# RMSNorm with GELU, one core: the first fill in three loads of 64 KB pieces, squares half a group ahead, and one store for the last group

## The chip, the cores and the metric

The kernel runs on one core of a Trainium2 chip. The metric is the device time of one execution in microseconds (us), fast runs only; a smaller number is better. "Faster" or "slower" asks for 2%, here 6.3 us. The profile of an execution covers its instructions from first to last (the span), some 1.8 us less than the time.

## The reference

x is 8 x 1024 x 2048 in float32: 8192 rows of 2048.

```python
rms = np.sqrt(np.mean(x ** 2, axis=-1, keepdims=True) + eps)
out = gamma * x / rms
return 0.5 * out * (1 + np.tanh(np.sqrt(2 / np.pi) * (out + 0.044715 * out ** 3)))
```

67.1 MB are read once and 67.1 MB written once. Nothing is reused but gamma.

## The kernel before

The rows are worked on in 16 groups of 512: each of 128 partitions holds four consecutive rows, 32 KB. Six buffers of that size (slots) go round: SyncE issues the loads, ScalarE squares the rows (accumulating a sum for each), GpSimd makes the inverse root from the four sums, VectorE multiplies by gamma in place, ScalarE applies GELU in place with the inverse root as its scale and issues the store. A load into a slot waits for the store that empties it.

```python
x3 = x...rearrange("(g p r) d -> g p r d", p=P, r=R)         # P = 128, R = 4
slot = [sbuf.tile([P, R, D], FP32, ...) for i in range(SLOTS)]   # 6
store_pieces = {
    0: [(R, [(0, NARROW), (NARROW, R * D)])],                # NARROW = 128 columns
    G - 1: [(1, [(r * D, r * D + D)]) for r in range(R)],    # the last group, row by row
}
...
for g in range(SLOTS):
    load(g)
...
for g in range(G + 1):
    if g < G:
        squares(g)                 # four ACTIVATE, one a row
        inverse_rms(g)             # six small GpSimd instructions
        scale(g)                   # one VectorE instruction (four for the last group)
    if g:
        gelu_store(g - 1)          # four ACTIVATE, then the store
        if g - 1 + SLOTS < G:
            load(g - 1 + SLOTS)
```

Squares of a whole group run ahead of the GELU of the one before. The first store is cut into a piece of 128 columns (512 bytes a partition) and the rest.

Of the kernel before, what the change touches and what calls it, by code (L numbers as in the profile page):

```python
# [1 line left out]

# [4 lines left out]

FP32 = mybir.dt.float32
ALU = mybir.AluOpType
ACT = mybir.ActivationFunctionType  # L10

P = 128
ROWS = 4
SLOTS = 6

GW = 32
CHUNK = 512

NARROW = 128


@with_exitstack
def kernel(
    ctx: ExitStack,
    tc: tile.TileContext,
    x: bass.AP,
    gamma: bass.AP,
    eps: bass.AP,
    out: bass.AP,
):  # L30




    nc = tc.nc
    D = x.shape[-1]
    R = ROWS
    eps_f = float(eps)
    x3 = x.rearrange("b s d -> (b s) d").rearrange("(g p r) d -> g p r d", p=P, r=R)
    o3 = out.rearrange("b s d -> (b s) d").rearrange("(g p r) d -> g p r d", p=P, r=R)  # L40
    G = x3.shape[0]

    sbuf = ctx.enter_context(tc.tile_pool(name="sbuf", bufs=1))
    psum = ctx.enter_context(
        tc.tile_pool(name="psum", bufs=1, space=bass.MemoryType.PSUM)
    )
    slot = [sbuf.tile([P, R, D], FP32, name=f"slot{i}") for i in range(SLOTS)]
    gamma_row = sbuf.tile([1, D // GW, GW + 4], FP32, name="gamma_row")
    ones = sbuf.tile([1, P], FP32, name="ones")
    warm = sbuf.tile([1, 1], FP32, name="warm")  # L50
    power = sbuf.tile([P, R], FP32, name="power")
    ssq = sbuf.tile([P, G, R], FP32, name="ssq")
    rstd = sbuf.tile([P, G, R], FP32, name="rstd")
    ms = sbuf.tile([P, R], FP32, name="ms")
    y = sbuf.tile([P, R], FP32, name="y")
    z = sbuf.tile([P, R], FP32, name="z")
    gamma_ps = psum.tile([P, D], FP32, name="gamma_ps")
    junk = psum.tile([P, D], FP32, name="junk")


    whole = [(R, [(0, R * D)])]
    store_pieces = {
        0: [(R, [(0, NARROW), (NARROW, R * D)])],
        G - 1: [(1, [(r * D, r * D + D)]) for r in range(R)],
    }
    scale_pieces = {G - 1: [(0, 1), (1, 1), (2, 1), (3, 1)]}

    def load(g):
        nc.sync.dma_start(out=slot[g % SLOTS], in_=x3[g])  # L69

    def squares(g):
        for r in range(R):
            nc.scalar.activation(  # L73
                out=junk,
                in_=slot[g % SLOTS][:, r, :],
                func=ACT.Square,
                accum_out=ssq[:, g, r : r + 1],
            )

    def scale(g):  # L80
        for r, n in scale_pieces.get(g, [(0, R)]):
            rows = slot[g % SLOTS][:, r : r + n, :]
            nc.vector.tensor_tensor(  # L83
                out=rows,
                in0=rows,
                in1=gamma_ps.unsqueeze(1).to_broadcast([P, n, D]),
                op=ALU.mult,
            )

    def inverse_rms(g):  # L90

        v = nc.gpsimd
        v.tensor_scalar(  # L93
            out=ms, in0=ssq[:, g, :], scalar1=1.0 / D, scalar2=eps_f,
            op0=ALU.mult, op1=ALU.add,
        )
        v.tensor_tensor(out=y, in0=ms, in1=power, op=ALU.pow)  # L97
        v.tensor_tensor(out=z, in0=y, in1=y, op=ALU.mult)  # L98
        v.tensor_tensor(out=z, in0=z, in1=ms, op=ALU.mult)  # L99
        v.tensor_scalar(  # L100
            out=z, in0=z, scalar1=-0.5, scalar2=1.5, op0=ALU.mult, op1=ALU.add
        )
        v.tensor_tensor(out=rstd[:, g, :], in0=z, in1=y, op=ALU.mult)  # L103

    def gelu_store(g):
        flat = slot[g % SLOTS].rearrange("p r d -> p (r d)")
        dst = o3[g].rearrange("p r d -> p (r d)")
        row = 0
        for n, stores in store_pieces.get(g, whole):
            for r in range(row, row + n):  # L110
                nc.scalar.activation(  # L111
                    out=slot[g % SLOTS][:, r, :],
                    in_=slot[g % SLOTS][:, r, :],
                    func=ACT.Gelu_apprx_tanh,
                    scale=rstd[:, g, r : r + 1],
                )
            row += n
            for a, b in stores:
                nc.scalar.dma_start(out=dst[:, a:b], in_=flat[:, a:b])  # L119

    with tc.manual_schedule():
        for k in range(0, D, CHUNK):
            nc.scalar.dma_start(
                out=gamma_row[:, k // GW : (k + CHUNK) // GW, 0:GW],
                in_=gamma[k : k + CHUNK].rearrange("(o a b) -> o a b", o=1, b=GW),
            )
        for g in range(SLOTS):
            load(g)
        nc.gpsimd.memset(power, -0.5)  # L129
        nc.vector.memset(warm, 0.0)  # L130
        nc.vector.memset(ones, 1.0)  # L131
        nc.scalar.activation(out=warm, in_=warm, func=ACT.Gelu_apprx_tanh)  # L132
        for k in range(0, D, CHUNK):
            nc.tensor.matmul(  # L134
                out=gamma_ps[:, k : k + CHUNK],
                lhsT=ones,
                rhs=gamma_row[:, k // GW : (k + CHUNK) // GW, 0:GW],
                start=True,
                stop=True,
            )  # L140
        for g in range(G + 1):
            if g < G:
                squares(g)
                inverse_rms(g)
                scale(g)
            if g:
                gelu_store(g - 1)
                if g - 1 + SLOTS < G:
                    load(g - 1 + SLOTS)


# [1 line left out]
_INS = ['x', 'gamma', 'eps']  # L153
_OUTS = [((8, 1024, 2048), 'float32')]

_NUMBERS = {'eps': 9.999999747378752e-06}


# [26 lines left out]
```

## Time and profile before

| | before |
|---|---|
| time | 317.41 us median of 3 (317.26 to 317.46) |
| span | 315.5 us |
| ScalarE / VectorE / GpSimd busy | 80% / 44% / 10% |
| DMA packets' time, share of 16 engines | 99.1% |
| first data packet, last packet | 1.73, 314.30 us |

The profile has one row for each instruction and a record for each packet that a DMA engine moved (queue, size, start, duration). Here a packet is one partition's contiguous run of bytes: 32 KB for a group's load. Each DMA also sends one 4-byte semaphore packet on each engine. The prediction shows the lines that matter, so here are only two marks that the change is going to shift. They are from the timeline of the kernel before (start, duration, engine, line, operation; in brackets the idle time before it), the first square and the last store:

```profile
13.47 1.88 ACT L73 ACTIVATE junk<-slot 128x2048 f32<-128x2048 f32 x1 [8.70 <-DMA slot<-in_x_dram]
...
297.05 0.34 ACTq L119 DMA_DIRECT2D out_dram<-slot  x1
```

The last store is issued at 297 us, but the queue is then so full that its last packet goes at 314.

### The profile page before, as it was taken

The page shows a single profiled execution, that of the slowest core. Times are in us where ns is not written, and L with a number is a line of the kernel's source. Part 1 is how long each engine was busy: PE and PEld are TensorE (multiplying, and loading weights), DVE is VectorE, ACT ScalarE, POOL GpSimd, SP SyncE. Part 2 cuts the span into 40 slices and gives each one's busy share as a digit, 9 for nine tenths or more (in the row PEclk, how much of TensorE's full clock was granted, in tenths as well). Part 3 has the DMA queues.
Part 4 walks back from the last instruction along what each step waited for, and adds up shares of the span by engine and source line. Part 5 has one row for each costly group of instructions (what it writes and reads, how often), then busy time and mean ns, then how long its engine had stood idle before and what let it go on. Part 6 is the DMA issues. An engine that isn't in the chain of part 4 may idle for free.

```text
span 315.5 us, 479 instructions
## 1 busy us (share of the span) xinstructions
PE 7.9 (3%) x8; PEld 2.1 (1%) x8; DVE 139.4 (44%) x21; ACT 251.2 (80%) x194; POOL 32.3 (10%) x101
## 2 busy tenths in 40 slices
PE   0810000000000000000000000000000000000000
PEld 0200000000000000000000000000000000000000
DVE  0028909091918282827328082370824609480000
ACT  1289999999999999989596895969959599598500
POOL 0020202020202020202020020200202002020000
DMA  8999999999999999999999999999999999999997
GB/s 329 404 461 403 459 413 396 453 406 462 403 461 407 457 407 458 411 453 416 449 428 440 432 432 432 432 440 424 446 416 453 411 453 411 453 415 449 416 418 314
DMA packets 5315, 134.25 MB, mean 426 GB/s; under 512 B 704, under 2 KB 832, under 8 KB 832
## 3 DMA queue, kind: packets, MB, share of 16 engines
q1 hardware_dynamic: 2304, 67.11, 49.7%
q10 hardware_dynamic: 3008, 67.12, 49.4%
q14 instruction: 3, 0.02, 0.0%
HBM read 67.12 MB, written 67.11 MB: 425 GB/s over the span
## 4 chain that ended last, share of the span: by engine, by line
ACT 38%; DMA 32%; another core or an unknown queue 18%; issue 5%; ACTq 1%; SPq 0%
ACT slot L111 21%; DMA slot<-in_x_dram 16%; ACT junk L73 16%; DMA out_dram<-slot 15%; ACTq L119 1%; SPq L69 0%; ACTq L111 0%; ACTq L73 0%
## 5 line engine op out<-in xcount | busy, mean ns | idle before, releaser
L83 DVE TENSOR_TENSOR slot<-slot,gamma_ps 128x8192 f32<-128x8192 f32 (+1 forms) x19 | 139.2, 7338 | 142.3 <-ACT junk L73 142.3
L73 ACT ACTIVATE junk<-slot 128x2048 f32<-128x2048 f32 x64 | 120.4, 1881 | 40.8 <-DMA slot<-in_x_dram 36.8
L111 ACT ACTIVATE slot<-slot,rstd 128x2048 f32<-128x2048 f32 x64 | 123.0, 1987 | 1.7 <-ACT slot L111 1.7
L93 POOL TENSOR_SCALAR ms<-ssq 128x4 f32<-128x4 f32 x16 | 3.1, 194 | 242.8 <-ACT junk L73 242.8
L97 POOL TENSOR_TENSOR y<-ms,power 128x4 f32<-128x4 f32 x16 | 16.1, 1009 | 1.3
L73 ACT ACTIVATION_READ_ACCUMULATOR junk<-slot 128x1 f32 x64 | 11.9, 186 | 0.0
L134 PE MATMUL gamma_ps<-gamma_row,ones 1*128 1x512 f32 x8 | 7.9, 1112 | 9.2 <-DMA gamma_row<-in_gamma_dram 9.2
L132 ACT ACT_TABLE_LOAD x1 | 1.3, 1283 | 3.3 <-issue 3.3
L99 POOL TENSOR_TENSOR z<-z,ms 128x4 f32<-128x4 f32 x16 | 3.2, 201 | 1.3
L103 POOL TENSOR_TENSOR rstd<-z,y 128x4 f32<-128x4 f32 x16 | 3.2, 200 | 1.3
L98 POOL TENSOR_TENSOR z<-y 128x4 f32<-128x4 f32 x16 | 3.2, 200 | 1.3
L100 POOL TENSOR_SCALAR z<-z 128x4 f32<-128x4 f32 x16 | 3.1, 195 | 1.4
L134 PEld LDWEIGHTS gamma_ps<-gamma_row,ones 1*128 1x128 f32 x8 | 2.1, 306 | 13.4 <-issue 8.7
L130 DVE MEMSET warm<- 1x1 f32 x1 | 0.1, 59 | 0.8 <-PEq L166 0.8
L132 ACT ACTIVATE warm<-warm 1x1 f32<-1x1 f32 x1 | 0.2, 203 | 0.0
L131 DVE MEMSET ones<- 1x128 f32 x1 | 0.2, 165 | 0.0
L129 POOL MEMSET power<- 128x4 f32 x1 | 0.1, 102 | 0.3 <-POOLq L166 0.3
L166 POOL MEMSET const-float32-0.0<- 128x1 f32 x1 | 0.1, 99 | 0.2 <-issue 0.2
L166 POOL MEMSET const-bfloat16-1.0<- 128x1 bf16 x1 | 0.1, 102 | 0.0
L166 POOL MEMSET const-uint8-127<- 128x1 uint8 x1 | 0.1, 102 | 0.0
L166 POOL MEMSET const-float32-1.0<- 128x1 f32 x1 | 0.1, 99 | 0.0
## 6 DMA issues: line engine op xcount, KB each, us to landing
slot<-in_x_dram SPq DMA_DIRECT2D x16, 4096.0 KB, 29.9
out_dram<-slot ACTq DMA_DIRECT2D x14, 4096.0 KB, 43.3
out_dram<-slot ACTq DMA_DIRECT2D x4, 1024.0 KB, 17.5
out_dram<-slot ACTq DMA_DIRECT2D x1, 4032.0 KB, 28.5
gamma_row<-in_gamma_dram ACTq DMA_DIRECT2D x4, 2.0 KB, 10.3
out_dram<-slot ACTq DMA_DIRECT2D x1, 64.0 KB, 14.4
```

What stands on the lines that cost most here:

```text
L73: nc.scalar.activation(out=junk, in_=slot[g % SLOTS][:, r, :], func=ACT.Square, accum_out=ssq[:, g, r : r + 1],)
L83: nc.vector.tensor_tensor(out=rows, in0=rows, in1=gamma_ps.unsqueeze(1).to_broadcast([P, n, D]), op=ALU.mult,)
L93: v.tensor_scalar(out=ms, in0=ssq[:, g, :], scalar1=1.0 / D, scalar2=eps_f, op0=ALU.mult, op1=ALU.add,)
L97: v.tensor_tensor(out=y, in0=ms, in1=power, op=ALU.pow)
L98: v.tensor_tensor(out=z, in0=y, in1=y, op=ALU.mult)
L99: v.tensor_tensor(out=z, in0=z, in1=ms, op=ALU.mult)
L100: v.tensor_scalar(out=z, in0=z, scalar1=-0.5, scalar2=1.5, op0=ALU.mult, op1=ALU.add)
L103: v.tensor_tensor(out=rstd[:, g, :], in0=z, in1=y, op=ALU.mult)
L111: nc.scalar.activation(out=slot[g % SLOTS][:, r, :], in_=slot[g % SLOTS][:, r, :], func=ACT.Gelu_apprx_tanh, scale=rstd[:, g, r : r + 1],)
L119: nc.scalar.dma_start(out=dst[:, a:b], in_=flat[:, a:b])
L132: nc.scalar.activation(out=warm, in_=warm, func=ACT.Gelu_apprx_tanh)
L134: nc.tensor.matmul(out=gamma_ps[:, k : k + CHUNK], lhsT=ones, rhs=gamma_row[:, k // GW : (k + CHUNK) // GW, 0:GW], start=True, stop=True,)
```

## The change

It has four parts. The six slots become three pairs, filled at the start by three loads of eight rows a partition (64 KB packets, half as many). The squares run half a group ahead instead of a whole one, with VectorE's scaling cut into halves (into single rows for the first and the last group). The last group leaves in one store, not in four. Gamma comes in two DMAs instead of four. The intent is fewer and larger packets, and a shorter way from a load to its store.

```diff
+    def part(a, g):
+        if g < SLOTS:
+            return pair_part(a, g // 2)[:, g % 2 * R : g % 2 * R + R, :]
+        return a[g * R * P : (g + 1) * R * P].rearrange("(p r) d -> p r d", p=P)
-    slot = [sbuf.tile([P, R, D], FP32, name=f"slot{i}") for i in range(SLOTS)]
+    pair = [sbuf.tile([P, 2 * R, D], FP32, ...) for i in range(SLOTS // 2)]
+    slot = [pair[i // 2][:, i % 2 * R : i % 2 * R + R, :] for i in range(SLOTS)]
...
-        G - 1: [(1, [(r * D, r * D + D)]) for r in range(R)],
...
-        for g in range(SLOTS):
-            load(g)
+        for k in range(SLOTS // 2):
+            nc.sync.dma_start(out=pair[k], in_=pair_part(x2, k))
...
-        for g in range(G + 1):
-            if g < G:
-                squares(g)
-                inverse_rms(g)
-                scale(g)
-            if g:
-                gelu_store(g - 1)
-                if g - 1 + SLOTS < G:
-                    load(g - 1 + SLOTS)
+        squares(0, 0, HALF)
+        for g in range(G):
+            squares(g, HALF, R - HALF)
+            inverse_rms(g)
+            step = 1 if g in (0, G - 1) else HALF
+            for r in range(0, R, step):
+                scale(g, r, step)
+            if g < G - 1:
+                squares(g + 1, 0, HALF)
+            gelu(g, 0, R)
+            store(g)
+            if g + SLOTS < G:
+                load(g + SLOTS)
```

The first store keeps its 512-byte piece.

More of the change, by code (lines that the diff above doesn't have):

```diff
@@ L13 @@
 ROWS = 4
+HALF = 2
 SLOTS = 6
-GW = 32
-CHUNK = 512
+GW = 64
+GAMMA = [(0, 1024), (1024, 2048)]
 NARROW = 128
@@ L38, with pair_part @@
     eps_f = float(eps)
-    x3 = x.rearrange("b s d -> (b s) d").rearrange("(g p r) d -> g p r d", p=P, r=R)
-    o3 = out.rearrange("b s d -> (b s) d").rearrange("(g p r) d -> g p r d", p=P, r=R)
-    G = x3.shape[0]
+    x2 = x.rearrange("b s d -> (b s) d")
+    o2 = out.rearrange("b s d -> (b s) d")
+    G = x2.shape[0] // (P * R)
+    def pair_part(a, k):
+        n = 2 * R * P
+        return a[k * n : (k + 1) * n].rearrange("(p r) d -> p r d", p=P)
+    def part(a, g):
+        if g < SLOTS:
+            return pair_part(a, g // 2)[:, g % 2 * R : g % 2 * R + R, :]
+        return a[g * R * P : (g + 1) * R * P].rearrange("(p r) d -> p r d", p=P)
     sbuf = ctx.enter_context(tc.tile_pool(name="sbuf", bufs=1))
@@ L46 @@
     )
-    slot = [sbuf.tile([P, R, D], FP32, name=f"slot{i}") for i in range(SLOTS)]
-    gamma_row = sbuf.tile([1, D // GW, GW + 4], FP32, name="gamma_row")
+    pair = [
+        sbuf.tile([P, 2 * R, D], FP32, name=f"pair{i}") for i in range(SLOTS // 2)
+    ]
+    slot = [pair[i // 2][:, i % 2 * R : i % 2 * R + R, :] for i in range(SLOTS)]
+    gamma_row = sbuf.tile([1, D // GW, GW + 8], FP32, name="gamma_row")
     ones = sbuf.tile([1, P], FP32, name="ones")
@@ L58, with store, squares, scale @@
     junk = psum.tile([P, D], FP32, name="junk")
-    whole = [(R, [(0, R * D)])]
-    store_pieces = {
-        0: [(R, [(0, NARROW), (NARROW, R * D)])],
-        G - 1: [(1, [(r * D, r * D + D)]) for r in range(R)],
-    }
-    scale_pieces = {G - 1: [(0, 1), (1, 1), (2, 1), (3, 1)]}
-    def load(g):
-        nc.sync.dma_start(out=slot[g % SLOTS], in_=x3[g])
-    def squares(g):
-        for r in range(R):
+    def load(g):
+        nc.sync.dma_start(out=slot[g % SLOTS], in_=part(x2, g))
+    def store(g):
+        if g:
+            nc.scalar.dma_start(out=part(o2, g), in_=slot[g % SLOTS])
+            return
+        src = pair[0].rearrange("p r d -> p (r d)")
+        dst = pair_part(o2, 0).rearrange("p r d -> p (r d)")
+        for a, z in ((0, NARROW), (NARROW, R * D)):
+            nc.scalar.dma_start(out=dst[:, a:z], in_=src[:, a:z])
+    def squares(g, r, n):
+        for q in range(r, r + n):
             nc.scalar.activation(
                 out=junk,
-                in_=slot[g % SLOTS][:, r, :],
+                in_=slot[g % SLOTS][:, q, :],
                 func=ACT.Square,
-                accum_out=ssq[:, g, r : r + 1],
+                accum_out=ssq[:, g, q : q + 1],
             )
-    def scale(g):
-        for r, n in scale_pieces.get(g, [(0, R)]):
-            rows = slot[g % SLOTS][:, r : r + n, :]
-            nc.vector.tensor_tensor(
-                out=rows,
-                in0=rows,
-                in1=gamma_ps.unsqueeze(1).to_broadcast([P, n, D]),
-                op=ALU.mult,
-            )
+    def scale(g, r, n):
+        rows = slot[g % SLOTS][:, r : r + n, :]
+        nc.vector.tensor_tensor(
+            out=rows,
+            in0=rows,
+            in1=gamma_ps.unsqueeze(1).to_broadcast([P, n, D]),
+            op=ALU.mult,
+        )
     def inverse_rms(g):
@@ L103, in inverse_rms, with gelu @@
         v.tensor_tensor(out=rstd[:, g, :], in0=z, in1=y, op=ALU.mult)
-    def gelu_store(g):
-        flat = slot[g % SLOTS].rearrange("p r d -> p (r d)")
-        dst = o3[g].rearrange("p r d -> p (r d)")
-        row = 0
-        for n, stores in store_pieces.get(g, whole):
-            for r in range(row, row + n):
-                nc.scalar.activation(
-                    out=slot[g % SLOTS][:, r, :],
-                    in_=slot[g % SLOTS][:, r, :],
-                    func=ACT.Gelu_apprx_tanh,
-                    scale=rstd[:, g, r : r + 1],
-                )
-            row += n
-            for a, b in stores:
-                nc.scalar.dma_start(out=dst[:, a:b], in_=flat[:, a:b])
+    def gelu(g, r, n):
+        for q in range(r, r + n):
+            nc.scalar.activation(
+                out=slot[g % SLOTS][:, q, :],
+                in_=slot[g % SLOTS][:, q, :],
+                func=ACT.Gelu_apprx_tanh,
+                scale=rstd[:, g, q : q + 1],
+            )
     with tc.manual_schedule():
-        for k in range(0, D, CHUNK):
+        for k in range(SLOTS // 2):
+            nc.sync.dma_start(out=pair[k], in_=pair_part(x2, k))
+        for a, b in GAMMA:
             nc.scalar.dma_start(
-                out=gamma_row[:, k // GW : (k + CHUNK) // GW, 0:GW],
-                in_=gamma[k : k + CHUNK].rearrange("(o a b) -> o a b", o=1, b=GW),
-            )
-        for g in range(SLOTS):
-            load(g)
+                out=gamma_row[:, a // GW : b // GW, 0:GW],
+                in_=gamma[a:b].rearrange("(o a b) -> o a b", o=1, b=GW),
+            )
         nc.gpsimd.memset(power, -0.5)
@@ L132 @@
         nc.scalar.activation(out=warm, in_=warm, func=ACT.Gelu_apprx_tanh)
-        for k in range(0, D, CHUNK):
+        for k in range(0, D, 512):
             nc.tensor.matmul(
-                out=gamma_ps[:, k : k + CHUNK],
+                out=gamma_ps[:, k : k + 512],
                 lhsT=ones,
-                rhs=gamma_row[:, k // GW : (k + CHUNK) // GW, 0:GW],
+                rhs=gamma_row[:, k // GW : (k + 512) // GW, 0:GW],
                 start=True,
```

## The prediction

> **What bounds the kernel now.** I read the views from the outside in: the page's slices and queue rows, then the waits, then the table of stretches, then single DMA packet records in the trace.
>
> ```profile
> DMA  8999999999999999999999999999999999999997
> GB/s 329 404 461 403 459 413 396 453 406 462 403 461 407 457 407 458 411 453 416 449 428 440 432 432 432 432 440 424 446 416 453 411 453 411 453 415 449 416 418 314
> ...
> q1 hardware_dynamic: 2304, 67.11, 49.7%
> q10 hardware_dynamic: 3008, 67.12, 49.4%
> ```
> q1 carries the loads, q10 the stores (and gamma). Their packets fill 49.7 + 49.4 = 99.1% of sixteen engines' span; only the first and last slices are below 9. The transfers are the bound from one end to the other.
>
> ```profile
> ACT junk L73 <- DMA slot<-in_x_dram: 36.8, 10, 8.7
> ...
> SPq L69 <- DMA out_dram<-slot: 224.3, 10, 53.7
> ```
> ScalarE waits for data (36.8 us in ten waits: 8.7 before the first group, later some 3.7 a group), and the load queue waits for stores to free a buffer. So the compute engines have slack, although ScalarE is 80% busy.
>
> ```profile
> L83 DVE TENSOR_TENSOR slot<-slot,gamma_ps 128x8192 f32<-128x8192 f32 x15 | 130.3, 8687 | 137.8 <-ACT junk L73 137.8
> L111 ACT ACTIVATE slot<-slot,rstd 128x2048 f32<-128x2048 f32 x64 | 123.0, 1987 | 1.7 <-ACT slot L111 1.7
> L73 ACT ACTIVATE junk<-slot 128x2048 f32<-128x2048 f32 x64 | 120.4, 1881 | 40.8 <-DMA slot<-in_x_dram 36.8 <-ACT slot L111 2.5
> L83 DVE TENSOR_TENSOR slot<-slot,gamma_ps 128x2048 f32<-128x2048 f32 x4 | 8.9, 2280 | 4.6 <-ACT junk L73 4.6
> ```
> One group costs ScalarE 16.1 us (stores are issued at 38.77, 54.86, 70.94: steps of 16.1). The same group costs DMA 8.39 MB / 433 GB/s = 19.4 us, and the trace's completions are indeed 19.36 us apart in the middle. 16.1 < 19.4 is the whole story of the steady state.
>
> ```profile
> 50.00:100.00 50.00, 0.00 (x0) 0.00 (x0) 27.80 (x4) 48.47 (x38) 6.00 (x18) 1.00 1.00 430
> 100.00:150.00 50.00, 0.00 (x0) 0.00 (x0) 27.40 (x4) 48.07 (x38) 6.00 (x18) 1.00 1.01 437
> ```
> The DMA share is 1.00 (last but one column). The packet records say the rest: first data packet at 1.73 us, last at 314.29, and 312.66 us of packet time per engine between them, so no gap. The mean rate is 433 GB/s in every ten microseconds but 0:10 and 40:50. The chain that ended last does not show this plainly: it wanders over ScalarE and a queue because it follows semaphores, not a full pipe.
>
> Hence time = 1.7 us of start + packet time per engine + about 1.2 us from the last packet to the end of the span + 1.7 us outside the span (317.24 against 315.5). Only packet time, or a new gap in it, can move the result.
>
> **What the Trainium skill says.**
> - "DMA: Bandwidth & Descriptors", section "Where 436 GB/s comes from": 435.2 GB/s is the fabric ceiling. The trace's 433 is 99.5% of it; the bytes do not change, so nothing large is left to win.
> - Same page, "Why small descriptors are slow (HBM only)": a fixed cost per packet. The trace agrees that there is one, and I use its size: packets of 512, 8192 and 32768 bytes take 0.027, 0.309 and 1.213 us. The slope is (1.213-0.309) us / 24576 B = 27.2 GB/s an engine, the intercept 8 ns; a semaphore packet takes 9 ns.
> - Same page, "Queues, rings and completion order": an engine takes a packet from each queue in turn. The trace agrees: here a packet is one row piece, and the 512-byte packets of the first small store run at 36.5, 37.7, 38.9, 40.1, ... us, one after each 1.21 us load packet.
> - "ScalarE: Activation LUTs", "What ACT_TABLE_LOAD costs": about 1990 ns for 2048 elements with a pointer operand. The trace has 1987. Splitting squares two and two adds no instruction, so ScalarE's work is unchanged.
>
> **The change part by part.**
>
> *Loads of 64 KB pieces.* Six loads of 8 packets an engine (48 of 1.213 us) become three with 24 of 2.418 (my estimate: 65536 B at the slope above plus 8 ns). Saved: 24 x 8 ns = 0.19 us. All of this is on the path, because the pipe is the path.
>
> *Fewer DMAs.* 40 DMAs (16 loads, 20 stores, 4 gamma) become 32 (13, 17, 2). Each costs an engine one semaphore packet: 8 x 9 ns = 0.07 us. Two gamma pieces fewer: about 0.02 us.
>
> *One whole last store.* 32 packets of 0.309 us an engine (9.89) become 8 of 1.213 (9.70): 0.18 us saved. It is only a gain if the store is issued before the queue runs dry, checked below.
>
> *First group later.* Before, the first load completed at 12.8 and ScalarE began at 13.47. Now 8 MB must land: 1.73 + 0.75 (the first packet of each engine took about 2.0 instead of 1.21) + 8 x 2.418 = 21.8, plus 1.3 of completion = 23.1. Then six squares of 2.03 (12.2) and four gelus (7.7): the first large store is issued near 43 instead of 38.8. That delay lies beside loads that still have work until 60 us, so it costs nothing.
>
> *Who gets the pipe from 40 to 70 us.* The 512-byte store is kept. Its 8 packets an engine now wait one 64 KB packet each: 8 x 2.42 = 19.4 us instead of 9.7. So the large first store begins when the first loads are nearly over, near 1.73 + 0.75 + 24 x 2.418 + 0.3 = 60.8 us. From there store 0 runs alone (9.55 us) to 70.4; store 1, issued near 60 (43 + 16.1), continues; load 6 joins near 72. At each moment one queue has work: no gap. At 72 us 6 groups are in and 1.2 out, a lead of 4.8 groups. Before, after the last load 314.29 - 271.24 = 43.05 us of stores were left, 43.05/9.70 = 4.4 groups of lead.
>
> *The end.* 4.8 x 9.70 = 46.6 us of stores left puts the last load at about 313.8 - 46.6 = 267 (271 before). ScalarE then needs 1.3 + 4.06 (two squares) + 7.7 + 0.4 (gelu and issue, group 14) + 4.06 + 2.4 (GpSimd's chain) + 7.7 = 27.6: the last store is issued near 295. The earlier stores occupy the queue to about 304. Slack about 9 us, so the whole store starves nothing. The half-group-ahead squares keep ScalarE from idling in GpSimd's 2.4 us, off the path.
>
> Sum: 0.19 + 0.07 + 0.02 + 0.18 = 0.46 us. 317.41 - 0.46 = 316.95; I say 316.9.
>
> **The rivals.**
> 1. *A gap at the hand-over near 60 us, or at the end.* Store 0 or store 1 comes late and the queue is dry. For: the first data reaches ScalarE 9.6 us later than before, and loads run in fewer, larger lumps. Against: store 0 is due 17 us before its need, store 1 about 10, the last one about 9. If it happened, 1 to 5 us: 318 to 322.
> 2. *64 KB pieces are slower than the slope says*, or the first three groups' stores (32 KB rows at a pitch of 64 KB) are. For: no packet of that size is in this trace. Against: row loads run at the fabric's pace whatever is beside them. 1% on a quarter of the traffic would be 0.8 us: 317.3.
> 3. *The loss at 40:50 changes.* Load packets from 45.1 to 48.4 us took up to 2.04 instead of 1.213, 0.67 us an engine in all, when the first full-size store packets begin. If it belongs to stores beginning beside loads, the change removes it because the loads are nearly over: 316.2. If it belongs to the beginning of stores, it stays. I take it as staying.
> 4. *The gain comes through ScalarE*, as the chain (38% ACT) suggests: the earlier squares shorten it by several us. The full pipe speaks against it: there is no time for stores to come forward into. It would make 312 or less, which 134.22 MB at 433 GB/s (310.0) plus 4.6 of ends nearly forbids.
>
> **Range and chances.** Small terms are fairly sure to about 0.1; the engines finish up to 1.0 us apart (last semaphore packets from 313.26 to 314.29) and that spread may shift by some tenths; rival 3 gives -0.7, rivals 1 and 2 give a tail upwards. So 316.1 to 317.6. Two per cent is 6.3 us: faster needs more than the pipe allows (0.01), slower needs a gap of over 6 us (0.02), within 2% has the rest, 0.97.
>
> **What would show it.** Right: load packets of 65536 B near 2.42 us; ScalarE's first square near 23; store 0's large part starting near 60; the last load near 267; no DMA slice under 9 between the ends; last store issued near 295, DMA ended near 313.8; waits of ScalarE for data fewer at the end (from about group 12 instead of 9). Wrong: any ten microseconds with DMA under 430 GB/s apart from the ends, packets of 64 KB above 2.45 us, or stores of groups 0 to 5 above 1.22 us a packet.

## The result, and the profile after

| | before | changed |
|---|---|---|
| time, median | 317.44 us (317.26 to 317.50, 4 runs) | 317.49 us (317.27 to 317.77, 4 runs) |
| ratio, 95% interval | | 1.0003 (0.9986 to 1.002) |
| second, 9 and 5 runs | 317.54 us | 317.56 us, 1.0002 (0.999 to 1.0015) |

A ratio is the mean time of one kernel's fast runs over that of the other's in the same rounds, so not quite the ratio of the medians quoted beside it. The change does nothing that the clock can see.

The page of the changed kernel, its slices of DMA busy tenths and rate, and its queues (packets, MB, share of sixteen engines):

```profile
DMA  9999999999999999999999999999999999999996
GB/s 399 399 399 424 507 403 402 385 405 461 404 461 407 461 403 461 408 457 407 457 415 449 432 432 432 432 440 421 449 415 449 415 453 411 453 412 449 415 453 282
DMA packets 4388, 134.26 MB, mean 425 GB/s; under 512 B 544, under 2 KB 672, under 8 KB 672
## 3 DMA queue, kind: packets, MB, share of 16 engines
q1 hardware_dynamic: 1872, 67.11, 49.7%
q10 hardware_dynamic: 2512, 67.12, 49.3%
q14 instruction: 4, 0.03, 0.0%
```

There are 432 load packets fewer (2304 to 1872) and 496 store packets fewer (3008 to 2512). The DMA slices are full up to the last and the shares are the same to 0.1%. Before, the last row read:

```profile
q14 instruction: 3, 0.02, 0.0%
```

The waits of the changed kernel (engine, line, what it waited for: us in total, times, longest):

```profile
ACT junk L92 <- DMA pair<-in_x_dram: 33.4, 6, 19.2
...
ACT pair L125 <- POOL rstd L121: 2.5, 1, 2.5
```

ScalarE waits for data 33.4 us instead of 36.8: one wait of 19.2 at the start and five, each of at most 3.5, from 192 us on. Its instructions and VectorE's, with different shapes kept apart (count, busy us, mean ns, idle time before):

```profile
L101 DVE TENSOR_TENSOR pair<-pair,gamma_ps 128x4096 f32<-128x4096 f32 x28 | 123.0, 4418 | 114.7 <-ACT junk L92 114.7
L125 ACT ACTIVATE pair<-pair,rstd 128x2048 f32<-128x2048 f32 x64 | 122.6, 1986 | 2.5 <-POOL rstd L121 2.5
L92 ACT ACTIVATE junk<-pair 128x2048 f32<-128x2048 f32 x64 | 120.4, 1881 | 41.0 <-DMA pair<-in_x_dram 33.4 <-ACT pair L125 6.2
```

The ScalarE groups are those of before to 0.4 us. The two marks of the timeline, now, with the issue of the first large store between them:

```profile
22.70 1.88 ACT L92 ACTIVATE junk<-pair 128x2048 f32<-128x2048 f32 x1 [19.21 <-DMA pair<-in_x_dram]
...
42.47 0.34 ACTq L88 DMA_DIRECT2D out_dram<-pair  x1
...
296.42 0.34 ACTq L83 DMA_DIRECT2D out_dram<-pair  x1
```

ScalarE starts 9.2 us later than before and ends 0.6 us earlier, while the last packet goes at 314.40 instead of 314.30 us.

**The balance of packet time.** I added up the packet records of loads, stores and gamma. "Undisturbed" is the number of packets of each size times the duration that nearly all of that size have (65536 B 2.418 us, 32768 B 1.213, 8192 B 0.309, 512 B 0.027, semaphore 0.009); "excess" is what single packets took beyond it; most of it is a lengthening of a few load packets, called the stall below. All are us per engine.

| kernel | packet time | undisturbed | excess | of it ahead of the first store packets | mean / last end of the engines |
|---|---|---|---|---|---|
| before | 312.66 | 311.19 | 1.47 | 0.67 | 313.56 / 314.30 |
| changed | 312.54 | 310.72 | 1.82 | 0.94 | 313.53 / 314.40 |

The undisturbed time fell by 0.47 us, as predicted (0.46). The excess rose by 0.35 and gave most of it back; the engine that ends last sets the time, and it did not gain.

The table leaves out one term. The records can be strung together by engine, and in them nearly every packet starts 3 or 4 ns before the packet ahead of it ends. A packet therefore takes some 3.5 ns less of the pipe than its record lasts. With 274 packets an engine instead of 332, this overlap shrinks by 58 x 3.5 ns = 0.20 us, so only about 0.27 of the 0.47 us could be saved. The sum -0.47 + 0.20 + 0.35 = +0.08 us fits what the engines show: from the mean start of their first packets to the mean of their ends they took 311.60 us before and 311.65 after.

The experiments ask whether that full pipe really is the whole bound, and where the excess sits.

### The profile page after: what moved, and what is told of

It is laid out like the page before. It is cut to its first block, busy times and chain, and to the rows that moved or that the text cites. A ratio compares the mean times of both kernels' runs of the same rounds, so it can differ in the third digit from the quotient of the medians.

```text
span 315.6 us, 504 instructions
## 1 busy us (share of the span) xinstructions
PE 7.5 (2%) x8; PEld 2.3 (1%) x8; DVE 141.0 (45%) x38; ACT 250.8 (79%) x194; POOL 32.1 (10%) x101
## 3 DMA queue, kind: packets, MB, share of 16 engines
q1 hardware_dynamic: 1872, 67.11, 49.7%
q10 hardware_dynamic: 2512, 67.12, 49.3%
## 4 chain that ended last, share of the span: by engine, by line
ACT 38%; DMA 31%; another core or an unknown queue 12%; issue 11%; ACTq 1%; POOL 1%; SPq 0%; POOLq 0%
ACT pair L125 22%; ACT junk L92 16%; DMA out_dram<-pair 16%; DMA pair<-in_x_dram 15%; ACTq L83 1%; POOL y L115 0%; SPq L79 0%; ACTq L88 0%; POOLq L195 0%; POOL z L117 0%; POOL z L116 0%; POOL ms L111 0%; POOL z L118 0%; ACTq L92 0%
## 5 line engine op out<-in xcount | busy, mean ns | idle before, releaser
L101 DVE TENSOR_TENSOR pair<-pair,gamma_ps 128x4096 f32<-128x4096 f32 (+1 forms) x36 | 140.8, 3944 | 146.9 <-ACT junk L92 146.9
L92 ACT ACTIVATE junk<-pair 128x2048 f32<-128x2048 f32 x64 | 120.4, 1881 | 41.0 <-DMA pair<-in_x_dram 33.4
L125 ACT ACTIVATE pair<-pair,rstd 128x2048 f32<-128x2048 f32 x64 | 122.6, 1986 | 2.5 <-POOL rstd L121 2.5
L115 POOL TENSOR_TENSOR y<-ms,power 128x4 f32<-128x4 f32 x16 | 16.1, 1008 | 1.3
L92 ACT ACTIVATION_READ_ACCUMULATOR junk<-pair 128x1 f32 x64 | 11.9, 186 | 0.0
```

The costliest lines, as they stand in the source:

```text
L92: nc.scalar.activation(out=junk, in_=slot[g % SLOTS][:, q, :], func=ACT.Square, accum_out=ssq[:, g, q : q + 1],)
L101: nc.vector.tensor_tensor(out=rows, in0=rows, in1=gamma_ps.unsqueeze(1).to_broadcast([P, n, D]), op=ALU.mult,)
L115: v.tensor_tensor(out=y, in0=ms, in1=power, op=ALU.pow)
L125: nc.scalar.activation(out=slot[g % SLOTS][:, q, :], in_=slot[g % SLOTS][:, q, :], func=ACT.Gelu_apprx_tanh, scale=rstd[:, g, q : q + 1],)
```

## The experiments

Theory A: the sixteen DMA engines are never idle between the ends, so only packet time counts. Theory B: ScalarE's path (first square, GELU, last store) counts. Each kernel below is the changed one with the edit shown; every one gave correct outputs.

### The first fill undone

```diff
-        for k in range(SLOTS // 2):
-            nc.sync.dma_start(out=pair[k], in_=pair_part(x2, k))
+        for g in range(SLOTS):
+            load(g)
```

> The changed kernel with its first fill undone to six loads of 32 KB pieces (same places in memory, so the pitch of 64 KB stays). Theory A (the DMA pipe is the bound, and only packet time counts): packet time per engine +0.19 us for 24 more data packets and +0.03 for three more semaphore packets, while the stall of the load packet before the first full-size store packet falls from 0.95 to about 0.67 us; ScalarE's first square comes back from 22.7 to about 13.5 us; the time stays within 0.4 us of the changed kernel (317.1 to 317.9). Theory B (the late first group costs time by way of ScalarE): about 4 us faster, since the first large store is issued about 4 us earlier.

317.66 us (317.47 to 317.72) against 317.45 for the kernel before, ratio 1.0007 (0.9992 to 1.0022). Undisturbed packet time 310.94 (+0.22), stall 0.86, packet time 312.59. From its timeline:

```profile
12.83 1.88 ACT L92 ACTIVATE junk<-pair 128x2048 f32<-128x2048 f32 x1 [9.34 <-DMA pair<-in_x_dram]
...
34.24 0.34 ACTq L88 DMA_DIRECT2D out_dram<-pair  x1
...
302.57 0.34 ACTq L83 DMA_DIRECT2D out_dram<-pair  x1
```

ScalarE starts ten microseconds earlier than in the changed kernel and the first large store is issued at 34.24 instead of 42.47 us, and its packets begin at 43.4 instead of 61.5 us, yet the last packet of all goes no earlier (314.50 against 314.40): B fails. One thing I had not looked for: the last load now completes at 275.76 instead of 269.62 us and the last store is issued at 302.57 instead of 296.42, while the earlier stores run dry at 304.81. The 64 KB first fill sends loads ahead of stores, and so gives the whole last store its slack (some 7 us against some 1).

### The first store in one piece

```diff
-        for a, z in ((0, NARROW), (NARROW, R * D)):
+        for a, z in ((0, R * D),):
```

> The changed kernel with the first store as one whole piece, without the 512-byte one ahead. Theory A (the stall belongs to the beginning of full-size stores on each engine): the stall of 0.7 to 1.0 us an engine stays and moves to about 46 us; packet time falls by 8 x 27 + 9 ns = 0.23 us; loads get two of three bytes from there on, the load queue ends near 72 instead of 62 us; time 317.0 to 317.6. Theory B (the small store or its semaphore packet causes the stall): the stall goes, packet time falls by about 1.2 us, time about 316.3.

317.95 us (317.58 to 319.7), ratio 1.0029 (0.9994 to 1.0063): unclear, with more scatter than any other kernel, and not in the range I gave. The stall stayed, 1.05 us, and moved to the load packets that start near 44 us, ahead of the first 32 KB store packets. So the small store does not cause it. A second loss of 0.34 us came near 86 us in the profiled execution, and one engine ended at 315.23. Why that loss and the scatter come without the small store is open.

### The last store undone

```diff
-            gelu(g, 0, R)
-            store(g)
+            if g < G - 1:
+                gelu(g, 0, R)
+                store(g)
+            else:
+                for r in range(R):
+                    gelu(g, r, 1)
+                    nc.scalar.dma_start(out=part(o2, g)[:, r : r + 1, :],
+                                        in_=slot[g % SLOTS][:, r : r + 1, :])
```

> The changed kernel with the last group's store undone to four stores of 8 KB pieces, each after its row. Theory A: packet time +0.18 us (32 x 0.309 instead of 8 x 1.213) and +0.03 us of semaphore packets; the first of them is issued near 291 instead of 296, which is hidden behind stores queued until 304.7; time +0.2 us, 317.5 to 317.9, not to be told apart by the clock. Theory B (the end of ScalarE's work sets the end, so early pieces help): 2 us or more faster.

317.83 us (317.68 to 318.09), ratio 1.0015 (1.0 to 1.003). Undisturbed packet time rose by 0.22, as it should; packet time was 312.62. The first piece was issued at 290.75 and had to wait until the stores before it ended at 304.72. B fails: early pieces help nothing.

### The squares a whole group ahead again

```diff
-        squares(0, 0, HALF)
+        squares(0, 0, R)
+        inverse_rms(0)
         for g in range(G):
-            squares(g, HALF, R - HALF)
-            inverse_rms(g)
...
-                squares(g + 1, 0, HALF)
+                squares(g + 1, 0, R)
+                inverse_rms(g + 1)
```

> The changed kernel with squares a whole group ahead as in the kernel before; everything else kept. Theory A: ScalarE's instruction order changes but no DMA packet does; packet time equal within 0.1 us, the first large store issued about 4 us later (near 47 us), which still lies beside the first loads; time within 0.3 us of the changed kernel. Theory B (the earlier gelus of the half-group lead are worth time): 4 us slower.

317.45 us (317.14 to 317.58), ratio 1.0001 (0.9986 to 1.0015). Packet time 312.55 against 312.54; the first large store was issued at 46.79, 4.3 us later. A's expectation to the letter: the new order of ScalarE's squares is worth nothing by itself (the halved scales were kept here).

### ScalarE delayed at the end, by a little and by a lot

```diff
+    spare = sbuf.tile([P, 16], FP32, name="spare")
...
+            if g == G - 1:
+                for i in range(3):        # 8 in the second run
+                    nc.scalar.activation(out=junk, in_=slot[g % SLOTS][:, i % R, :],
+                        func=ACT.Square, accum_out=spare[:, i : i + 1])
             gelu(g, 0, R)
```

> The changed kernel with three more squares (2.03 us each, into a spare tile; the outputs stay right) just before the last group's gelus. The last gelus now wait 2.5 us for GpSimd, which the first of them fill, so the last store is issued about 6.1 - 2.5 = 3.6 us later, near 300 instead of 296.4. Theory A (stores in the queue until 304.7 us hide it): no change, 317.1 to 317.8. Theory B (ScalarE's end sets the time): +3.6 us, 321.

> The same with eight more squares: the last store is issued 16.2 - 2.5 = 13.7 us later, near 310. Theory A: the queue runs dry at 304.7 us; the last store's first packet starts about 2 us after its issue, near 312, so the gap is 7.5 us and the time about 325 (323.5 to 326), half of the delay being hidden. Theory B: +13.7 us, 331.

One run each; the kernel before took 317.35 us on the same chip. With three extra squares: 317.31 us, no change, though the last store was issued 3.4 us later:

```profile
299.85 0.34 ACTq L84 DMA_DIRECT2D out_dram<-pair  x1
```

With eight: 324.08 us, 6.7 more than before, with the store issued at 310.37, 13.95 us later. The stretches of that run (length, busy time and count by engine, clock, DMA share, GB/s):

```profile
295.00:305.00 10.00, 0.00 (x0) 0.00 (x0) 0.00 (x0) 9.90 (x10) 0.00 (x0) 1.00 0.86 370
305.00:311.00 6.00, 0.00 (x0) 0.00 (x0) 0.00 (x0) 5.34 (x3) 0.00 (x0) 1.00 0.00 0
311.00:322.00 11.00, 0.00 (x0) 0.00 (x0) 0.00 (x0) 0.00 (x0) 0.00 (x0) 1.00 0.89 381
```

From 305 to 311 us the DMA moves nothing. The stores before ended at 305.02, the last store's first packet went at 311.21: a gap of 6.2 us, nearly the whole loss. A store's first packet went 0.84 us after its issue here, so in the changed kernel the slack is 304.71 - (296.42 + 0.84) = 7.4 us. Both runs fit this slack: 3.4 us of delay cost nothing, and of 13.95 us the part over it, some 6.5, was paid in full (6.7 measured). The state of these single runs is unknown, but no granted clock was below 1.0 and the kernel before ran as always.

### ScalarE delayed at the start

The same edit with four squares and `g == 0`.

> The changed kernel with four more squares just before the first group's gelus: every store of the first groups is issued up to 8.1 us later (minus any wait they fill), the first large one near 50 us and the second near 66. Theory A (needed only when the first loads end near 62 and the first store near 71): no gap and no change, 317.1 to 317.9. Theory B (ScalarE's start sets the time): +8.1 us, 325.5.

317.56 us against 317.35, one run. The first large store was issued at 50.65, 8.2 us later than in the changed kernel, and completed at 71.75 instead of 71.66 us. The delay vanished in the time in which the first loads have the pipe.

### Where the stall belongs

In the changed kernel each engine has one load packet near 58 us that takes 3.0 to 3.7 us instead of 2.418; it is the last load packet of the first fill, and the next packet on that engine is its first 31.5 KB store packet. Put in a row by start and end, the packets of one engine read (L load, S store, bytes @ start + duration; my own listing of the records):

```
S512@55.79+0.03 ... S4@58.20+0.01 L65536@58.20+3.48 S32256@61.68+1.20 L4@62.87+0.01 S32256@62.88+1.19
```

The following run made the small piece 2048 columns wide (8 KB packets):

```diff
-NARROW = 128
+NARROW = 2048
```

> The changed kernel with the first store's small piece 2048 columns wide (8 KB a row instead of 512 bytes). It tells where the stall of 0.95 us belongs. If it belongs to the first store packets of any real size, it moves to the load packets ahead of the first 8 KB store packets, near 41 us, and the ones near 58 go. If it belongs to the step to the large pieces, or to the small store's semaphore packet, it stays ahead of the first 24 KB packet, near 60 us. Packet time otherwise changes by 8 x 8 ns at most; time 317.1 to 317.9 either way.

317.07 us against 317.35, one run. Of the stall 0.54 us moved to the load packets that start near 39 us, just ahead of the first 8 KB store packets; 0.16 was left near 60, ahead of the first 24 KB ones. Timed with five rounds, beside the changed kernel again:

> The changed kernel once more, for a narrower interval beside the next ones. Packet time per engine 312.4 to 312.7 us, of which the stall ahead of the first full-size store packets about 0.95; the median within 0.2 us of the kernel before.

> The changed kernel with 8 KB pieces in the small first store, timed: the single look had stalls of 0.54 + 0.16 us at two places instead of 0.94 at one. If that repeats (theory: a smaller first store packet pays less of the one-time stall), packet time is about 0.25 us below the changed kernel's and the median about 317.1 to 317.3. If it was chance, no difference.

The changed kernel had 317.56 us (317.32 to 317.77) and a stall of 1.01. The wide one had 317.20 (317.15 to 317.32), and 0.26 + 0.56 us of stall (near 39 and near 60): 312.30 us of packet time against 312.56. The means are 317.23 and 317.55, ratio 0.9990. Against the kernel before of the same rounds it is 0.9993 (0.9979 to 1.0007). A saving of 0.26 to 0.29 us shows in the packet records both times, but by the clock it can't be told from the kernel before.

How the stall splits did not repeat: 0.54 + 0.16 us in the first profile, 0.26 + 0.56 in the second, 0.35 + 0.37 in the kernel with whole scales below, whose first store is the same. So it did not simply move. What all the profiles share is where nearly all of it sits: on the one or two load packets of an engine ahead of its first packets of a store of kilobytes, in these three at the beginning of both such stores. The end of the first fill doesn't explain it: without the small store it comes near 44 us and with the fill undone near 41, while these fills last to 67 and 79. Stores of 512 bytes begin without it (41 us in the changed kernel). With the first fill undone, though, 12 engines have part of it one load packet earlier, ahead of the last 512-byte packet.

I took the smaller packets for the reason, and tested it with a third piece:

```diff
-        for a, z in ((0, NARROW), (NARROW, R * D)):
+        for a, z in ((0, NARROW), (NARROW, D), (D, R * D)):
```

> The changed kernel with the first store in three pieces (512 B, 7.5 KB and 24 KB a row). One more DMA costs an engine 8 x 8 + 9 = 0.07 us. If the stall is paid by the first store packets of kilobytes and less by small ones, it is again 0.5 to 0.7 us in all, most of it ahead of the 7.5 KB packets near 58 us or later, and the time is about 0.2 us below the changed kernel's; if it is paid once whatever the size, 0.95 us and the time unchanged.

317.55 us (317.44 to 317.62), ratio 1.0001 (0.9989 to 1.0014). The stall was 1.06 us, all ahead of the 7.5 KB packets, which started near 61.6. Packets of 7.5 KB paid in full, so packet size alone is not what made the wide store cheaper. What differs there is that its packets begin near 42 us, one between two load packets each; whether that is the reason, and what the engine does in the stall, stays open.

### One instruction fewer a group, and a bound that came back

```diff
-NARROW = 128
+NARROW = 2048
-            step = 1 if g in (0, G - 1) else HALF
+            step = 1 if g in (0, G - 1) else R
```

> The same, and VectorE scales groups 1 to 14 in one instruction each, as before the change: 14 instructions fewer. Theory: the instruction queue then moves three pieces of 8 KB during the run as before, not four; each piece holds one DMA engine up by 0.31 us and no other, so it matters only if it falls on the engine that ends last. Expected: three pieces, the spread of the engines' ends no more than now (0.9 us), time 0 to 0.3 us below the changed kernel. Rival: the order of VectorE's work is on the path, then 2 us or more slower, for the gelus wait for it.

364.1 us (364.04 to 364.14), ratio 1.1468 (1.1453 to 1.1484). My theory looked at a hundredth of this (the instruction queue did move three pieces, as expected); the rival was right, and much more than the 2 us I had given it. Its page (DMA slices) and its waits:

```profile
DMA  8998999999999999999999999998999255280948
```

```profile
ACT pair L125 <- DVE pair L101: 66.5, 14, 4.7
```

One group in its timeline of ScalarE, from one store to the next:

```profile
105.35 0.34 ACTq L83 DMA_DIRECT2D out_dram<-pair  x1
...
113.65 0.19 ACT L92 ACTIVATION_READ_ACCUMULATOR junk<-pair 128x1 f32 x1
118.58 7.68 ACT L125 ACTIVATE pair<-pair,rstd 128x2048 f32<-128x2048 f32 x4 [4.75 <-DVE pair L101]
126.29 0.34 ACTq L83 DMA_DIRECT2D out_dram<-pair  x1
```

A whole-group scale takes 8.69 us and can't start before the group's last square; only two squares (4.1 us) lie between that and the GELU. So ScalarE waits 4.75 us in each of 14 groups, and its period becomes 126.29 - 105.35 = 20.9 us instead of 16.1. That is over the 19.36 us that DMA needs for a group, and ScalarE becomes the bound: stores come too late, and the last slices of the DMA row fall to 2, 5, 5, 2, 8, 0. With squares a whole group ahead, as before, the four squares (8.1 us) cover nearly all of such a scale. The halved scales are not a detail: squares half a group ahead need them.

## Why the prediction was right or wrong, point by point

- **The bound** was right. The undoing of the first fill, the last store and the squares left the time within 0.2% with intervals that reach 1 (the last store's undoing is at most 0.3% slower; gamma's DMAs were not undone), and ScalarE's start could move by 8 us and its end by 3.4 us without effect, until its slack was used up (the eight squares) or its period passed 19.36 us (the whole scales). One reading behind it was loose: 312.66 us of packet records don't prove that there is no gap, for they are more than the 312.56 us from the first to the last. Strung together by engine, the records of the changed kernel show that there is none.
- **The sum of 0.46 us** was right as the length of the records: 311.19 to 310.72 undisturbed, and 0.22 of it came back when the fill or the last store was undone. As time in the pipe it was mis-sized: it took a record's 8 ns of fixed cost for the gain of a packet saved, while the records overlap by 3.5 ns, so that about 0.27 us was to be had. Packets of 64 KB took 2.418 us, the estimate to the nanosecond; rival 2 is dead. (Its 317.3 does not follow from its own 0.8 us either: 316.9 + 0.8 = 317.7, over the range.)
- **Rival 3, "I take it as staying", is the other mis-sized term.** The stall stayed, but measured 0.94 us in the changed kernel (0.90 to 1.16 in its variants with the same fill and small store) instead of 0.67. With the fill undone it was 0.86. One profile of each varies by about 0.1, so that the 64 KB pieces are the whole reason is not shown. The other profit went into the overlap (0.20 us) and 0.08 of other excess; the mean end went from 313.56 to 313.53, the last from 314.30 to 314.40. The stall also put two stretches of ten microseconds under 430 GB/s, 414 from 50 to 60 us and 412 from 60 to 70 (each packet's bytes spread over its duration; 401 from 40 to 50 before): the prediction's own sign of being wrong, which a stall that stays was bound to set off.
- **The result,** 317.49, is 0.6 us over the point and inside the range. That says little: no change at all, 317.41, lay inside it too, and a gain of 0.46 us would lie outside the second interval (ratio 0.999 at the least, some 0.3 us).
- **First group and hand-over:** first square 22.70 (23.1 predicted), first large store issued at 42.47 (43), its packets from 61.5 (60.8). No gap, as said; rival 1 did not occur.
- **The lead of 4.8 groups** was too large. Load 6 was issued at 72.11, but its first packet went only at 76.0, while store packets ran (why it waited is not shown), so stores caught up: (314.40 - 269.62)/9.68 = 4.6 groups. The last load therefore completed at 269.62, not 267.
- **The end:** last store issued at 296.42 (295), earlier stores done at 304.71 (304), slack 7.4 us measured with the help of the eight squares (9).
- **Rival 4**, ScalarE's chain, was rejected rightly, and sq_undo settles it. ScalarE's waits for data came three groups later than before, as said (from group 11 instead of 8).

## What to carry to other kernels

When the packets of the DMA engines fill the span, count packets, bytes and one-time stalls, a packet by the time from its start to the next one's start and not by its record, and judge every reordering of the compute engines by its slack only: their period against that of the transfers (16.1 against 19.36 us here) and the time at which the last store is needed. A long slack hides a harmless change and a harmful one alike until one of these two is crossed, as the whole scales did at once with 47 us. Larger first loads shift the order in the queues more than the cost: they put loads ahead, which buys slack at the end (7 instead of 1 us) rather than time.

## What the Trainium skill lacked or had wrong

- A one-time stall at the beginning of stores: load packets just ahead of an engine's first store packets of kilobytes are longer by 0.67 us in all before and 0.94 in the changed kernel (0.70 to 1.16 in its variants, sometimes split over two stores). Its cause is open. No page has it.
- "DMA: Bandwidth & Descriptors", section "Queues, rings and completion order", has packets of 9 to 17 descriptors as typical. In these traces each partition's run is its own packet, up to 65536 bytes in 2.418 us, and two queues alternate one for one: 512-byte store packets follow each other at 1.23 us between 32 KB loads and at 2.44 us between 64 KB ones.
- Same page, "Why small descriptors are slow (HBM only)", gives the fixed cost per packet in cycles; in these traces the records have 8 ns at every size from 512 B to 64 KB and overlap by 3.5 ns, so doubling a 32 KB packet (2.4145 us instead of 2 x 1.2095) wins 0.2% of the time.
- "Runtime: NRT & Kernel Launch", section "Instruction fetch mechanics", has blocks of 16 KiB, mostly hidden. Here the instruction queue moved pieces of 8 KB within the span, three before and four changed, each taking one data engine 0.31 us in a pipe that has no free time. In both profiles of the changed kernel the engine that ends last (314.40 and 314.57 us; the first is 0.87 after the mean end) is the one that carries two of the four pieces, and the packet after each of the two was 0.25 to 0.34 us longer than usual. So the pieces cost that engine some 1.2 us, enough to make it the last; no run took them away.
